# First layer's down projection of four quads as seven block products, x chunks in pairs, PSUM in two tiles of four banks

## Chip, core and metric

The kernel runs on one core of a Trainium2 chip. The metric is the device time of one execution in microseconds (us), as the median of three runs. The engines are named as in the profile: PE multiplies matrices and PEld loads its weights beside it, DVE and ACT work on vectors, POOL and SP are used here to issue transfers. PE's results land in PSUM, a memory of eight banks of 512 float32 words on each of 128 partitions; DVE or ACT read them from there (an "evacuation" below) into the on-chip buffer SBUF.

## What is computed

Two layers of a bidirectional encoder over 512 tokens of width 1024. Each layer has two attention branches fed by one input projection, and then a gated feed-forward part of hidden width 2816, which the change is about:

```python
for l in range(DEPTH):                       # DEPTH = 2
    h = rms_norm(x, attn_norm_g[l])
    z = jnp.einsum('bsd,dc->bsc', h, w_in[l])
    ...
    x = x + jnp.einsum('bsd,de->bse', mixed, w_out[l])
    h = rms_norm(x, ffn_norm_g[l])
    u = jax.nn.silu(jnp.einsum('bsd,df->bsf', h, w_gate[l])) * jnp.einsum('bsd,df->bsf', h, w_up[l])
    x = x + jnp.einsum('bsf,fd->bsd', u, w_down[l])
```

All is float32. Each product of matrices is made of three passes of the reduced type float32r: both operands are split in a high and a low part, and high x high, high x low and low x high are added up in PSUM.

## The kernel before

**How the work is tiled.** x lies with its features on partitions in eight chunks of 128 features x 512 tokens (`xT`), so a plain product has 128x128 weights and 512 tokens of moving data: three matmuls of 512 columns for each 128x128 weight block. In the feed-forward part the first 256 hidden features are done plainly (`pair_matmul`), and the other 2560 as five "quads" of 512. A quad's gate and up projections are made with seven block products instead of eight (2x2 blocks of 512 x 256 weights and 512 x 256 tokens, with sums of blocks ahead of the products and of results behind): `m_step` runs one product, 24 matmuls of 256 columns. The class `Quad` loads a quad's weights, makes the sums of weight blocks, and splits each in a high and a low part.

**The down projection.** In the first layer it is plain: `d_products` takes one chunk c of 128 output features and the four feature blocks of a quad, 12 matmuls of 512 columns with the tokens as moving data, and `add_x` adds the bank to `xT[c]`. Eight such steps make one quad. In the last layer it is made with seven block products too (`d_step`, letter "D"), with tokens on partitions: 12 matmuls of 512 columns for one product, evacuated by two additions. `chain_v` makes the sums and the split of the hidden blocks for it.

**What sets the order.** The whole program is unrolled by a planner: the kernel function runs `trunk` twice, once dry with a clock for each engine, to choose the places of the buffers and the order, and once to emit instructions. The main line (`layer`) emits PE's matmuls in order. Short chains (attention, splits) are emitted between them when their inputs are due (`Need`, `issue`). What follows a product, its evacuation among it, is put off with `soon` by 0.1 us of the planner's clock, and `tick` then emits it after the next three matmuls. `token_steps` and `ffn_steps` list the order of the steps in the last and in the first layer.

**PSUM.** `bank()` takes one bank's worth of words out of one tile of eight banks (`ARENAS`, kind `PS`); `Layout.pack` gives it a place after the dry run. The framework on which the kernel is built adds the waits between engines by itself, from what each instruction reads and writes in a tile. Attention holds at most four banks at once by a count of slots (`at_slots`); the other banks are used by the projections and by the feed-forward part. All calculating instructions are emitted through one helper, so the profile shows them with one line (L337), and buffers are named "arena".

Of the kernel before, what the change touches and what calls it, by code (L numbers as in the profile page):

```python
# [29 lines left out]
ARENAS = {F32: 21504, F32R: 31104, PS: 8 * 512}  # L30
# [197 lines left out]
def trunk(ctx: ExitStack, tc: tile.TileContext, a: dict, out: bass.AP, lay: Layout):  # L228
# [8 lines left out]
    def nm(s):  # L237
# [4 lines left out]
        k: (pb if k == PS else ar).tile([P, lay.WORDS if lay.dry else n], F32 if k == PS else k, tag=f"ar{i}", name=f"arena{i}")  # L242
# [21 lines left out]
    def bank():  # L264
        return buf([S], PS)
# [261 lines left out]
    def token_steps():  # L527

        steps = []
        for q in range(QUADS):  # L530
            ms = [("m", q, w, m) for w in ("w_gate", "w_up") for m in ORDER]
            ds = [("D", q - 1, m) for m in DORDER] if q else [("t", *x) for x in np.ndindex(2, NB)]
            for i, m in enumerate(ms):
                steps.append(m)
                for _ in range(i % 2 if q else 2 * (i >= 5)):
                    if ds:
                        steps.append(ds.pop(0))
        return steps + [("D", QUADS - 1, m) for m in DORDER]

    def ffn_steps():  # L540
        groups = [(0, 2)] + [(2 + 4 * i, 4) for i in range(QUADS)]
        steps = []
        for q in range(QUADS):
            ms = [("m", q, w, m) for w in ("w_gate", "w_up") for m in ORDER]
            ds = [("d", *groups[q], c) for c in range(KD)]
            for i, m in enumerate(ms):
                steps.append(m)
                if ds and i >= (1 if q else 5):
                    steps.append(ds.pop(0))
        return steps + [("d", *groups[-1], c) for c in range(KD)]  # L550
# [3 lines left out]
    def plan_ffn(l):  # L554
        plan_pair(a["w_gate"][l], 0, KD, on_engines=True)
        plan_pair(a["w_up"][l], 0, KD)
        down = a["w_down"][l]
        for step in ffn_steps() if l < DEPTH - 1 else token_steps():
            if step[0] == "m":
                _, q, w, m = step  # L560
                if m == ORDER[0]:
                    t = total[0]
                    early = 18.0 if q == 0 and w == "w_gate" else 0.0
                    col = 256 + 512 * q
                    srcs = [a[w][l][512 * h : 512 * h + 512, col : col + 512] for h in range(2)]
                    quads[l, q, w] = Quad(srcs, t - early, early > 0.0, l == DEPTH - 1)
# [3 lines left out]
            elif step[0] == "D":  # L570
                _, q, m = step
                if m == DORDER[0]:
                    f0 = 256 + 512 * q
                    srcs = [down[f0 + 256 * h : f0 + 256 * h + 256] for h in range(2)]
                    early = LEAD_LAST if q == QUADS - 1 else 0.0
                    quads[l, q, "w_down"] = Quad(srcs, total[0] - early, False, True)
                quads[l, q, "w_down"].due(m, total[0] - early)
                at_pos(total[0] - LEAD_V, lambda key=("go", q, m): done.add(key))
                total[0] += 4 * UNIT
# [78 lines left out]
    class Quad:  # L658
# [3 lines left out]
        def __init__(self, srcs, t, first, transfers):  # L662
# [5 lines left out]
            if not self.paced:  # L668
                at_pos(t - LEAD_PREP - LEAD_RAW, self.load)

        def load(self):
            k, n = self.shape
            wide = [buf([k, 2 * n]) for _ in range(2)]
            for t, src in zip(wide, self.srcs):
                Q.dma_start(t, src)
            (self.a11, self.a21), (self.a12, self.a22) = ((t[:, :, :n], t[:, :, n:]) for t in wide)
            self.s1 = buf(self.shape)
            if self.first:
                spawn(self.chain())
# [8 lines left out]
        def due(self, m, t):  # L688
            if self.first:
                at_pos(t - LEAD_PREP, lambda: done.add((self, m)))  # L690
            elif not self.paced:
                at_pos(t - LEAD_PREP, lambda: (self.sums(m), self.high(m)))
                at_pos(t - LEAD_PREP + 1.8, lambda: self.low(m))
# [24 lines left out]
        def source(self, m):  # L718
            if self.paced:
                at = {1: (1, 1), 2: (1, 2), 4: (2, 2), 7: (2, 1)}  # L720
                return self.blocks[at[m]] if m in at else self.s2 if m == 6 else self.s1
            return {1: self.a11, 2: self.a12, 3: self.a12, 4: self.a22, 5: self.s1, 6: self.a11, 7: self.a21}[m]

        def sums(self, m):
            add = lambda o, x, y: V.tensor_tensor(o, x, y, ALU.add)
            if self.paced:
# [24 lines left out]
        def low(self, m):  # L751
            src, h = self.parts[m]
            lo = buf(self.shape, F32R)
            if self.paced and m in MOVED or self.first and m not in (1, 2):
# [58 lines left out]
    def turn_over(n):  # L813

        ps = bank()
# [47 lines left out]
    ps = bank()  # L863
# [11 lines left out]
    def chain_tables():  # L875
# [4 lines left out]
        ps = bank()  # L880
# [66 lines left out]
    class Norm:  # L947
# [18 lines left out]
        def chain(self):  # L966
# [4 lines left out]
            ps = bank()  # L971
# [10 lines left out]
            ps = bank()  # L982
# [8 lines left out]
    def pair_matmul(parts, xh, xl, evac):  # L991

        ps = [bank(), bank()]
# [16 lines left out]
    def token_matmul(nrm, evac, begin=None):  # L1010

        ps = [bank() for _ in range(NB)]
# [87 lines left out]
    def turned(tiles, col, perm):  # L1100

        at_slots.take()
        ps = bank()
# [4 lines left out]
    def turned_back(tiles, col):  # L1108

        at_slots.take()  # L1110
        ps = bank()
# [98 lines left out]
    def head(g, q, k, v, bias, perm, init, sink, o_dst, in_a, key):  # L1210
# [6 lines left out]
        for j in range(NB):  # L1217
# [4 lines left out]
            ps = bank()  # L1222
# [25 lines left out]
        for i, (turns, n, products, ends) in enumerate(steps_):  # L1248
# [3 lines left out]
            pt = bank()  # L1252
# [12 lines left out]
            if po is None:  # L1265
                at_slots.take()
                po = bank()
# [47 lines left out]
    def start(nrm, k):  # L1315

        done.add(f"x{k}")
        ps = bank()
# [16 lines left out]
    def layer(l):  # L1335
# [26 lines left out]
        def chain_kv():  # L1362
# [4 lines left out]
            for t in (kt, vt):  # L1367
                yield Need("pe", [t], [at_slots])
                at_slots.take()
                ps = bank()  # L1370
# [219 lines left out]

        nrm = norms[2 * l + 1] = Norm(2 * l + 1)
# [24 lines left out]
        def chain_out():  # L1616

            yield Need(keys=["x_out", f"rows{nrm.i}"])
            for b in range(NB):
                xo.append(buf([D]))  # L1620
                for half in range(2):
# [3 lines left out]
                    ps = bank()  # L1625
# [92 lines left out]
        def quadrant(q, w, i, t, src, sign):  # L1718
# [10 lines left out]
            if last:  # L1729
                blocks[q, i, t] = g.rearrange("p (j n) -> p j n", j=2)  # L1730
                done.add(("u", q, i, t))
# [10 lines left out]
        def chain_v(q):  # L1742
# [7 lines left out]
            def low(m):  # L1750
# [5 lines left out]
                done.add(("v", q, m))  # L1756

            def go(m, i, t):
                yield Need(keys=[("u", q, i, t), ("go", q, m)])
# [41 lines left out]
        def m_step(q, w, m):  # L1801
            if m == 1:
                ps.clear()
                if w == "w_up" and last:
                    spawn(chain_v(q))
                elif w == "w_up":
                    us[q] = [(buf([2, S], F32R), buf([2, S], F32R)) for _ in range(2)]
                    u.extend((hs[:, j], ls[:, j]) for hs, ls in us[q] for j in range(2))
# [14 lines left out]
            def seed():  # L1823
                ps["b"] = bank()
# [10 lines left out]
            def seed_c():  # L1835
                ps["c"] = plus(bank())
# [33 lines left out]
        def t_step(half, b, wk):  # L1870
            o = bank()
# [13 lines left out]
        def d_step(q, m):  # L1885
            at = "D" if m in (1, 6, 7, 4) else "E"
            if m in (1, 5, 2):
                pd[at] = [bank() for t in range(2)]
# [4 lines left out]
            for t in range(2):  # L1893
                pieces = [(pd[at][t], slice(0, S))]
                if final and m == DORDER[-1] and t:
                    pieces = [(pd[at][t], slice(0, S // 2)), (bank(), slice(S // 2, S))]
# [21 lines left out]

        if last:
            fluid[0] = True  # L1920
            spawn(chain_out())
            for i, step in enumerate(token_steps()):
# [17 lines left out]
                else:  # L1940
                    _, q, m = step
                    yield ("v", q, m)
# [3 lines left out]
        steps_ = ffn_steps()  # L1946
        for i, step in enumerate(steps_[:-KD]):
            if step[0] == "m":
# [4 lines left out]
                yield from m_step(q, w, m)  # L1953
            else:
# [6 lines left out]
                o = bank()  # L1961
# [3 lines left out]
        norms[2 * l + 2] = Norm(2 * l + 2)  # L1965
        for c in range(0, KD, 2):
            wk = w_take()
            os_ = [bank(), bank()]
            for half in range(2):
                for j in range(2):  # L1970
                    fs = range(f0 + 2 * half, f0 + 2 * half + 2)
# [38 lines left out]
```

## Time and profile before

| | |
|---|---|
| median of three runs | 1364.15 us (1364.15 to 1364.66) |
| the profiled execution | 1363.46 us, span 1361.7 us |
| PE busy | 1355.1 us (100% of the span), 8008 matmul records |
| PEld | 1202.9 us (88%) |
| DVE | 961.3 us (71%) |
| ACT | 774.5 us (57%) |
| POOL | 310.3 us (23%) |
| DMA | 219.00 MB, mean 161 GB/s |
| clock granted to PE | full in all 40 slices of the span |

The span is the time from the first to the last instruction in the profile. "Busy" is the time in which the engine had at least one instruction under way; matmuls are pipelined, so a single one lasts longer than its distance to the next one. The profile names what ended an engine's idle time ("idle before <- releaser"). The stages of the span are, in us: attention and projections of the first layer 0 to 367, its feed-forward part 367 to 694, the same of the second layer 694 to 1045 and 1045 to 1362.

### The profile page before, as it was taken

The page shows a single profiled execution, that of the slowest core. Times are in us where ns is not written, and L with a number is a line of the kernel's source. Part 1 is how long each engine was busy: PE and PEld are TensorE (multiplying, and loading weights), DVE is VectorE, ACT ScalarE, POOL GpSimd, SP SyncE. Part 2 cuts the span into 40 slices and gives each one's busy share as a digit, 9 for nine tenths or more (in the row PEclk, how much of TensorE's full clock was granted, in tenths as well). Part 3 has the DMA queues.
Part 4 walks back from the last instruction along what each step waited for, and adds up shares of the span by engine and source line. Part 5 has one row for each costly group of instructions (what it writes and reads, how often), then busy time and mean ns, then how long its engine had stood idle before and what let it go on. Part 6 is the DMA issues. An engine that isn't in the chain of part 4 may idle for free.

```text
span 1361.7 us, 21050 instructions
## 1 busy us (share of the span) xinstructions
PE 1355.1 (100%) x8008; PEld 1202.9 (88%) x8008; DVE 961.3 (71%) x1778; ACT 774.5 (57%) x1244; POOL 310.3 (23%) x325
## 2 busy tenths in 40 slices
PE   9999999999999999999999999999999999999998
PEld 7888888888899999999988888888888999999997
DVE  6876878455976566575648758784559587878888
ACT  7477677534643443333544766775347556667572
POOL 5442222300211010102244422223002111011110
PEclk9999999999999999999999999999999999999999
DMA  9997888873866373736799879879647877595873
GB/s 235 197 169 133 149 163 161 170 201 99 152 155 150 101 189 96 193 69 140 138 204 193 157 134 169 160 141 188 171 120 147 201 179 180 161 247 132 219 171 99
DMA packets 193188, 219.00 MB, mean 161 GB/s; under 512 B 26160, under 2 KB 159712, under 8 KB 193088
## 3 DMA queue, kind: packets, MB, share of 16 engines
q0 software_dynamic: 118816, 142.59, 55.5%
q1 hardware_dynamic: 73776, 74.40, 18.4%
q8 instruction: 63, 1.03, 0.3%
q10 hardware_dynamic: 496, 0.67, 0.2%
q14 instruction: 37, 0.30, 0.1%
HBM read 183.02 MB, written 2.10 MB: 136 GB/s over the span
## 4 chain that ended last, share of the span: by engine, by line
PE 91%; DVE 3%; ACT 2%; DMA 1%; issue 1%; POOL 1%; SPq 0%; ACTq 0%; POOLq 0%
PE arena L337 91%; DVE arena L337 2%; ACT arena L337 2%; DMA arena<-in_w_in 1%; POOL arena L337 1%; DMA arena<-in_rel_bias_b 0%; DVE sm L337 0%; DMA arena<-in_x 0%; ACT L337 0%; SPq L337 0%; ACT sm L337 0%; DVE den L337 0%; ACT trig L337 0%; DVE rstd L337 0%; ACTq L337 0%
## 5 line engine op out<-in xcount | busy, mean ns | idle before, releaser
L337 PE MATMUL arena<-arena 128*128 128x256 f32 (+2 forms) x7466 | 1323.3, 338 | 0.6 <-DVE arena L337 0.4
L337 PEld LDWEIGHTS arena<-arena 128*128 128x128 f32 x7466 | 1142.7, 190 | 141.9 <-issue 0.7
L337 DVE TENSOR_TENSOR arena<-arena,arena 128x512 f32<-128x512 f32 (+6 forms) x701 | 537.9, 792 | 290.9 <-PE arena L337 222.6
L337 ACT CAST arena<-arena 128x1024 fp32r<-128x1024 f32 (+4 forms) x443 | 341.5, 792 | 270.3 <-DVE arena L337 204.5
L337 ACT ACTIVATE arena<-arena 128x1024 fp32r<-128x1024 f32 (+3 forms) x302 | 247.0, 838 | 131.3 <-PE arena L337 40.6
L337 POOL DMA_DIRECT2D arena<-in_w_in x163 | 162.9, 1399 | 298.4 <-ACT arena L337 286.3
L337 DVE TENSOR_TENSOR arena<-arena 128x1024 f32<-128x1024 f32 (+3 forms) x226 | 189.3, 853 | 2.3
L337 ACT COPY arena<-arena 128x512 f32<-128x512 f32 (+1 forms) x118 | 67.9, 583 | 81.0 <-PE arena L337 78.7
L337 POOL DMA_DIRECT2D arena<-in_w_down x52 | 54.6, 1239 | 256.1 <-ACT arena L337 169.7
L337 POOL DMA_DIRECT2D arena<-arena x52 | 48.2, 926 | 268.1 <-ACT arena L337 167.8
L337 ACT ACTIVATE arena<-arena,negm 128x256 f32<-128x256 f32 (+1 forms) x128 | 68.2, 533 | 18.2 <-DVE negm L337 16.3
L337 PE MATMUL arena<-cst,arena 128*128 128x128 f32 x472 | 72.0, 273 | 1.7 <-DMA arena<-in_x 1.1
L337 PEld LDWEIGHTS arena<-cst,arena 128*128 128x128 f32 x472 | 57.2, 140 | 11.3 <-DVE arena L337 1.9
L337 DVE CUSTOM_DVE_ANT_0 arena<-arena,cst,nsnk 128x256 f32<-128x256 f32 (+1 forms) x64 | 34.4, 548 | 33.0 <-PE arena L337 32.2
L337 DVE CUSTOM_DVE_ANT_0 arena<-arena,arena 128x256 f32<-128x256 f32 x64 | 26.3, 420 | 20.9 <-PE arena L337 20.5
L337 ACT ACTIVATE arena<-arena,vec2T 128x512 fp32r<-128x512 f32 x16 | 11.6, 726 | 47.5 <-DVE arena L337 47.5
L337 POOL DMA_DIRECT2D arena<-in_w_up x8 | 8.3, 1035 | 125.4 <-PE arena L337 92.7
L337 DVE TENSOR_SCALAR arena<-arena,sm 128x256 f32<-128x256 f32 (+1 forms) x88 | 29.6, 387 | 1.1
L337 POOL DMA_DIRECT2D arena<-in_w_proj_b x16 | 17.5, 1286 | 50.9 <-ACT arena L337 50.9
L337 DVE TENSOR_REDUCE sm<-arena 128x8 f32<-128x512 f32 (+1 forms) x32 | 17.4, 579 | 16.3 <-ACT arena L337 16.3
L337 ACT ACTIVATE arena<-arena,sm 128x256 f32<-128x256 f32 (+1 forms) x40 | 20.0, 521 | 7.8 <-DVE sm L337 7.7
L337 ACT ACTIVATION_READ_ACCUMULATOR arena<-arena,negm 128x1 f32 x128 | 24.1, 188 | 0.0
(62 smaller groups left out, 262.8 us busy)
## 6 DMA issues: line engine op xcount, KB each, us to landing
arena<-in_w_in POOLq DMA_DIRECT2D x99, 512.0 KB, 7.3
arena<-arena POOLq DMA_DIRECT2D x52, 512.0 KB, 6.9
arena<-in_w_down POOLq DMA_DIRECT2D x44, 512.0 KB, 6.7
arena<-in_w_in POOLq DMA_DIRECT2D x64, 256.0 KB, 6.8
arena<-in_w_gate SPq DMA_DIRECT2D x12, 1024.0 KB
arena<-in_w_gate SPq DMA_DIRECT2D x20, 512.0 KB
arena<-in_w_up SPq DMA_DIRECT2D x10, 1024.0 KB
arena<-in_w_up SPq DMA_DIRECT2D x20, 512.0 KB
```

Of the source, the lines that this page charges most:

```text
L337: f(*args, **kw)
```

## The change

Four things are changed together.

- The first layer's down projection of quads 0 to 3 is made of seven block products (letter "F", `f_step`). Features stay on partitions: one product is 24 matmuls of 256 columns with sums of hidden blocks as moving data, in two banks, each of which a subtraction or addition of 128 x 512 puts into a pair of x chunks. `chain_v` makes the hidden blocks and `Quad` the weight blocks, as the last layer has them. The first 256 features and the last quad of that layer stay plain.
- The quads' weights of the first layer, but for the first, are loaded block by block, and three of the seven low parts are made by transfers that add (`low_by_transfer`), as in the last layer.
- The chunks of the first layer's new x lie in pairs in one buffer (`xp`).
- PSUM is two tiles of four banks in place of one of eight: "mm" for the projections and part of the feed-forward part, "at" for attention and the rest of the feed-forward part.

The core of the diff (each other `bank()` becomes `at_bank()` in the chains of attention and in `Norm`, and `mm_bank()` in `pair_matmul`, `token_matmul`, `t_step` and `d_products`):

```diff
-ARENAS = {F32: 21504, F32R: 31104, PS: 8 * 512}
+ARENAS = {F32: 21504, F32R: 31104, "mm": 4 * 512, "at": 4 * 512}
...
-        k: (pb if k == PS else ar).tile([P, lay.WORDS if lay.dry else n], F32 if k == PS else k, tag=f"ar{i}", name=f"arena{i}")
+        k: (pb if isinstance(k, str) else ar).tile([P, lay.WORDS if lay.dry else n], F32 if isinstance(k, str) else k, tag=f"ar{i}", name=f"arena{i}")
...
-    def bank():
-        return buf([S], PS)
+    def mm_bank():
+        return buf([S], "mm")
+
+    def at_bank():
+        return buf([S], "at")
...
+            if q:
+                ds = [("D" if last else "F", q - 1, m) for m in DORDER]
+            else:
+                ds = [("t", *x) for x in np.ndindex(2, NB)] if last else [("d", 0, 2, c) for c in range(KD)]
...
-            self.paced = transfers and not first
...
                 if l < DEPTH - 1:
-                    V.tensor_tensor(xT[k], xT[k], ps, ALU.add)
+                    if j == 0:
+                        xp.append(buf([2, S]))
+                    V.tensor_tensor(xp[dp][:, j], xT[k], ps, ALU.add)
+                    xT[k] = xp[dp][:, j]
...
             if m in (1, 5):
-                ps[at] = bank()
+                ps[at] = at_bank()
...
             def seed():
-                ps["b"] = bank()
+                ps["b"] = mm_bank()
                 A.copy(ps["b"], o)
...
-                ps["c"] = plus(bank())
+                ps["c"] = plus(mm_bank())
...
+        def f_step(q, m):
+            at = "D" if m in (1, 6, 7, 4) else "E"
+            if m in (1, 5, 2):
+                pd[at] = [(mm_bank if at == "D" else at_bank)() for p in range(2)]
+            hi, lo = quads[l, q, "w_down"].parts[m]
+            h, lw = vs[q, m]
+            half, th = DBLOCK[m]
+            for p in range(2):
+                o = pd[at][p]
+                for j, k in np.ndindex(2, 2):
+                    oj, c = o[:, 256 * j : 256 * j + 256], slice(P * (2 * p + j), P * (2 * p + j) + P)
+                    mm(oj, hi[:, k, c], h[:, k], m in (1, 5, 2) and j == k == 0, False)
+                    mm(oj, hi[:, k, c], lw[:, k], False, False)
+                    mm(oj, lo[:, k, c], h[:, k], False, k == 1)
+                    tick(3 * 0.12)
+                    yield UNIT
+
+                def add(o=o, p=p):
+                    x = xp[2 * half + p][:, :, 256 * th : 256 * th + 256]
+                    ps = o.rearrange("p (j n) -> p j n", j=2)
+                    V.tensor_tensor(x, x, ps, ALU.add if half == 0 else ALU.subtract)
+
+                soon(add)
```

Outside the first layer's feed-forward part the order of the instructions on each engine is the same but for a handful that change places; what differs there is the banks and the waits. In the rows below, which are PE's order with the semaphores that an instruction waits for (`DVE_49`, `Activation_49`, and `DMA...` for transfers), arena0 and arena1 are SBUF (float32 and float32r). Before, `arena2_71` is PSUM; of the change, `arena2_71` is the tile "mm" and `arena3_72` the tile "at".

First place: PE in the middle of the output projection `w_out` of the first layer, where two banks take turns, 12 matmuls each. Before:

```order
L337 MATMUL arena2_71<-arena1_70 128x512 [waits Activation_49]
L337 MATMUL arena2_71<-arena1_70 128x512 [waits DVE_49]
L337 MATMUL arena2_71<-arena1_70 128x512 x13
L337 MATMUL arena2_71<-arena1_70 128x512 [waits Activation_49]
L337 MATMUL arena2_71<-arena1_70 128x512
```

The same place of the change:

```order
L340 MATMUL arena2_71<-arena1_70 128x512 [waits Activation_49]
L340 MATMUL arena2_71<-arena1_70 128x512 [waits DVE_49]
L340 MATMUL arena2_71<-arena1_70 128x512
L340 MATMUL arena2_71<-arena1_70 128x512 [waits DVE_49]
L340 MATMUL arena2_71<-arena1_70 128x512 x11
```

A wait for DVE now stands at the first matmul of the second bank's last 12: the operation it waits for reads the first bank.

Second place: PE in the first layer's feed-forward part, at quad 1's products with one step of the down projection between them. Before:

```order
L337 MATMUL arena2_71<-arena1_70 128x256 x21
L337 MATMUL arena2_71<-arena1_70 128x512 x12
L337 MATMUL arena2_71<-arena1_70 128x256 [waits Activation_49]
L337 MATMUL arena2_71<-arena1_70 128x256
L337 MATMUL arena2_71<-arena1_70 128x256 [waits DVE_49]
L337 MATMUL arena2_71<-arena1_70 128x256 x21
```

The first F step of the change (24 matmuls), and the product behind it:

```order
L340 MATMUL arena2_71<-arena1_70 128x256 [waits DVE_49]
L340 MATMUL arena2_71<-arena1_70 128x256
L340 MATMUL arena2_71<-arena1_70 128x256 [waits DMASW6_49]
L340 MATMUL arena2_71<-arena1_70 128x256 x12
L340 MATMUL arena2_71<-arena1_70 128x256 [waits DVE_49]
L340 MATMUL arena2_71<-arena1_70 128x256 x11
L340 MATMUL arena2_71<-arena1_70 128x256 [waits DVE_49]
L340 MATMUL arena2_71<-arena1_70 128x256 x20
```

12 matmuls of 512 columns became 24 of 256, and there are waits for DVE three matmuls into the second bank's half of the step and three matmuls into the next product: after each evacuation that `soon` puts there.

Third place: PE in the second layer's feed-forward part, one D step (12 matmuls of 512 columns) and the start of the product behind it, code that the diff leaves as it was but for the banks. Before:

```order
L337 MATMUL arena2_71<-arena1_70 128x512 [waits Activation_49]
L337 MATMUL arena2_71<-arena1_70 128x512 [waits DVE_49]
L337 MATMUL arena2_71<-arena1_70 128x512 x10
L337 MATMUL arena2_71<-arena1_70 128x256 [waits DVE_49]
L337 MATMUL arena2_71<-arena1_70 128x256
L337 MATMUL arena2_71<-arena1_70 128x256 [waits DMASW2_49]
L337 MATMUL arena2_71<-arena1_70 128x256 x21
```

The same step of the change:

```order
L340 MATMUL arena2_71<-arena1_70 128x512 [waits Activation_49]
L340 MATMUL arena2_71<-arena1_70 128x512 x2
L340 MATMUL arena2_71<-arena1_70 128x512 [waits Activation_49]
L340 MATMUL arena2_71<-arena1_70 128x512 x5
L340 MATMUL arena2_71<-arena1_70 128x512 [waits DVE_49]
L340 MATMUL arena2_71<-arena1_70 128x512 x2
L340 MATMUL arena2_71<-arena1_70 128x256 x2
L340 MATMUL arena2_71<-arena1_70 128x256 [waits DMASW1_49]
L340 MATMUL arena2_71<-arena1_70 128x256 [waits DVE_49]
L340 MATMUL arena2_71<-arena1_70 128x256 x20
```

The matmuls are the same; waits for ACT and DVE stand three matmuls into the step, three into its second bank and three into the next product.

More of the change, by code (lines that the diff above doesn't have):

```diff
@@ L525, in trunk, with ffn_steps @@
     DORDER = (1, 5, 6, 3, 7, 4, 2)
-    def token_steps():
+    def ffn_steps(l):
+        last = l == DEPTH - 1
         steps = []
@@ L531, in token_steps @@
             ms = [("m", q, w, m) for w in ("w_gate", "w_up") for m in ORDER]
-            ds = [("D", q - 1, m) for m in DORDER] if q else [("t", *x) for x in np.ndindex(2, NB)]
+            if q:
+                ds = [("D" if last else "F", q - 1, m) for m in DORDER]
+            else:
+                ds = [("t", *x) for x in np.ndindex(2, NB)] if last else [("d", 0, 2, c) for c in range(KD)]
             for i, m in enumerate(ms):
                 steps.append(m)
-                for _ in range(i % 2 if q else 2 * (i >= 5)):
+                for _ in range(i % 2 if q else (i >= 5) * (1 + last)):
                     if ds:
                         steps.append(ds.pop(0))
[L538 to L550, printed above, removed]
+        q = QUADS - 1
+        return steps + ([("D", q, m) for m in DORDER] if last else [("d", 2 + 4 * q, 4, c) for c in range(KD)])
     quads = {}
@@ L557, in plan_ffn @@
         down = a["w_down"][l]
-        for step in ffn_steps() if l < DEPTH - 1 else token_steps():
+        for step in ffn_steps(l):
             if step[0] == "m":
@@ L575, in plan_ffn @@
                     early = LEAD_LAST if q == QUADS - 1 else 0.0
-                    quads[l, q, "w_down"] = Quad(srcs, total[0] - early, False, True)
+                    quads[l, q, "w_down"] = Quad(srcs, total[0] - early, False)
                 quads[l, q, "w_down"].due(m, total[0] - early)
-                at_pos(total[0] - LEAD_V, lambda key=("go", q, m): done.add(key))
-                total[0] += 4 * UNIT
+                at_pos(total[0] - LEAD_V, lambda key=("go", l, q, m): done.add(key))
+                total[0] += 4 * UNIT if kind == "D" else 24 * 0.12
             elif step[0] == "t":
@@ L677, in load @@
             self.s1 = buf(self.shape)
-            if self.first:
-                spawn(self.chain())
+            spawn(self.chain())
         def fetch(self, *blocks):
@@ L718, in source @@
         def source(self, m):
-            if self.paced:
+            if not self.first:
                 at = {1: (1, 1), 2: (1, 2), 4: (2, 2), 7: (2, 1)}
@@ L725, in sums @@
             add = lambda o, x, y: V.tensor_tensor(o, x, y, ALU.add)
-            if self.paced:
+            if not self.first:
                 at = self.blocks
@@ L753, in low @@
             lo = buf(self.shape, F32R)
-            if self.paced and m in MOVED or self.first and m not in (1, 2):
+            if m not in (1, 2) if self.first else m in MOVED:
                 low_by_transfer(lo, src, h)
@@ L813, in turn_over @@
     def turn_over(n):
-        ps = bank()
+        ps = mm_bank()
         for _ in range(n):
@@ L862, in trunk @@
     turn_over(7)
-    ps = bank()
+    ps = at_bank()
     T.transpose(ps[:, :16], vec, ident[:16, :16])
@@ L879, in chain_tables @@
         at_slots.take()
-        ps = bank()
+        ps = at_bank()
         T.transpose(ps[:, :P], vec2, ident)
@@ L970, in chain @@
             at_slots.take()
-            ps = bank()
+            ps = at_bank()
             for b in range(NB):
@@ L981, in chain @@
             at_slots.take()
-            ps = bank()
+            ps = at_bank()
             for b in range(NB):
@@ L1010, in token_matmul @@
     def token_matmul(nrm, evac, begin=None):
-        ps = [bank() for _ in range(NB)]
+        ps = [mm_bank() for _ in range(NB)]
         if begin is not None:
@@ L1102, in turned @@
         at_slots.take()
-        ps = bank()
+        ps = at_bank()
         for b in range(NB):
@@ L1110, in turned_back @@
         at_slots.take()
-        ps = bank()
+        ps = at_bank()
         for b in range(NB):
@@ L1251, in head @@
             th_slots.take()
-            pt = bank()
+            pt = at_bank()
             for j, x, to in turns:
@@ L1317, in start @@
         done.add(f"x{k}")
-        ps = bank()
+        ps = at_bank()
         for b in range(NB):
@@ L1728, in quadrant @@
                 V.scalar_tensor_tensor(g, src, sign, g, ALU.mult, ALU.mult)
-            if last:
+            if last or q < QUADS - 1:
                 blocks[q, i, t] = g.rearrange("p (j n) -> p j n", j=2)
-                done.add(("u", q, i, t))
+                done.add(("u", l, q, i, t))
                 return
@@ L1755, in low @@
                 vs[q, m] = h, lo
-                done.add(("v", q, m))
+                done.add(("v", l, q, m))
             def go(m, i, t):
-                yield Need(keys=[("u", q, i, t), ("go", q, m)])
+                yield Need(keys=[("u", l, q, i, t), ("go", l, q, m)])
                 return blocks[q, i, t]
@@ L1803, in m_step @@
                 ps.clear()
-                if w == "w_up" and last:
+                if w == "w_up" and (last or q < QUADS - 1):
                     spawn(chain_v(q))
@@ L1870, in t_step @@
         def t_step(half, b, wk):
-            o = bank()
+            o = mm_bank()
             t = slice(P * b, P * b + P)
@@ L1887, in d_step @@
             if m in (1, 5, 2):
-                pd[at] = [bank() for t in range(2)]
+                pd[at] = [(mm_bank if at == "D" else at_bank)() for t in range(2)]
             hi, lo = quads[l, q, "w_down"].parts[m]
@@ L1953, in layer @@
                 yield from m_step(q, w, m)
+            elif step[0] == "F":
+                _, q, m = step
+                yield ("v", l, q, m)
+                yield from f_step(q, m)
             else:
@@ L1965, in layer @@
         norms[2 * l + 2] = Norm(2 * l + 2)
+        fluid[0] = False
         for c in range(0, KD, 2):
             wk = w_take()
-            os_ = [bank(), bank()]
+            os_ = [mm_bank(), mm_bank()]
             for half in range(2):
                 for j in range(2):
-                    fs = range(f0 + 2 * half, f0 + 2 * half + 2)
+                    fs = range(2 + 2 * half, 4 + 2 * half)
                     yield from d_products(os_[j], c + j, fs, wk[2 * half : 2 * half + 2], half == 0, half == 1)
```

38 lines of the change are left out of this document (18 added, 20 removed).

## Prediction

> **What bounds the kernel now.** I read the page first: busy shares, the chain that ended last, and the costliest groups.
>
> ```profile
> span 1361.7 us, 21050 instructions
> PE 1355.1 (100%) x8008; PEld 1202.9 (88%) x8008; DVE 961.3 (71%) x1778; ACT 774.5 (57%) x1244; POOL 310.3 (23%) x325
> ...
> PE 91%; DVE 3%; ACT 2%; DMA 1%; issue 1%; POOL 1%; SPq 0%; ACTq 0%; POOLq 0%
> ...
> L337 PE MATMUL arena<-arena 128*128 128x256 f32 (+2 forms) x7466 | 1323.3, 338 | 0.6 <-DVE arena L337 0.4
> ```
>
> PE is busy all the time, the chain runs through it for 91% of the span, and the 7466 main matmuls waited 0.6 us altogether before they could start. So nothing else bounds this kernel, no evacuation of PSUM holds PE up today, and two things alone can change the time: the work that PE is given, and waits that PE does not have now.
>
> Next I read the windows of the steady stages: one quad of the first layer's feed-forward part with its step of the down projection, a stretch of 168 matmuls of 256 columns without any of 512, one quad of the second layer, and the gate projections of the first layer.
>
> ```profile
> core 0: us, PE busy (x) PEld busy (x) DVE busy (x) ACT busy (x) POOL busy (x), PEclk, DMA share, GB/s
> 427.35:489.59 62.24, 62.24 (x434) 58.33 (x432) 38.79 (x42) 24.02 (x30) 8.12 (x8) 1.00 0.57 133
> 466.69:486.84 20.15, 20.15 (x169) 20.15 (x168) 17.22 (x20) 7.33 (x9) 2.05 (x2) 1.00 0.45 105
> 1109.20:1168.70 59.50, 59.50 (x421) 56.07 (x420) 48.51 (x58) 38.46 (x45) 7.71 (x9) 1.00 0.73 186
> 253.00:348.00 95.00, 95.00 (x422) 78.66 (x420) 52.40 (x71) 43.79 (x63) 12.91 (x13) 1.00 0.64 152
> ```
>
> The columns are the window, its length, then busy time and instructions of each engine, the granted clock, and the DMA. PE is gapless in all of them. 20.15 us / 168 = 0.120 us for a matmul of 256 columns; 95.00 / 420 = 0.226 us for one of 512.
>
> **Term A, PE's own work.** A quad of the first layer is 336 matmuls of 256 columns (14 products x 24) and 96 of 512 (8 chunks x 4 blocks x 3): the 432 weight loads of the first window, 62.24 us. With seven products of 24 in place of the 96 it is 504 matmuls of 256 columns, 504 x 0.1199 = 60.45 us. That saves 1.79 us a quad, 4 x 1.79 = 7.2 us for four. An eighth less of the 22 us of those 96 would be 2.7 us; the shorter matmuls, at more than half the distance of the long ones, take back the rest. It is the whole gain that the change can have.
>
> What comes with it on the other engines: for each of four quads seven splits of hidden blocks and their sums, four sums and seven splits of weight blocks, and 14 evacuations instead of 8. The second layer does all of this already, in the third window: DVE 48.51 us of 59.50, ACT 38.46, DMA share 0.73, and PE without a gap. The first layer has the same products in 60.45 us, so I cost these edits at nothing; they would cost only if DVE ran full, for which 11 us a quad are left. Pairs of x chunks in one buffer move no instruction. The three low parts that now come by adding transfers stand on the queues in the same third window, with PE fed.
>
> **Term B, the new waits.** The order shows something that the diff does not. With one PSUM tile of eight banks, each wait of PE for DVE or ACT that concerns PSUM was for an operation on the same bank. In the order of the change, with two tiles of four banks, I count 566 waits of PE for an evacuation, a seed or another operation of DVE or ACT that touches *another* bank of the same tile; before there are none. 376 are for DVE, 190 for ACT. By stage: first layer ahead of its feed-forward part 166, that part 119, second layer ahead of its feed-forward part 156, that part 125. In 387 of them (89, 102, 90, 106) the waiting matmul stands right behind the last matmul that the evacuation itself has to wait for, with nothing between; `soon` puts most evacuations three matmuls into the next step, and the fourth then waits. In the other 179 PE has work on the other tile in between.
>
> The price of one, from the groups by shape:
>
> ```profile
> L337 PE MATMUL arena<-arena 128*128 128x512 f32 x3582 | 866.8, 393 | 0.1
> L337 DVE TENSOR_TENSOR arena<-arena,arena 128x512 f32<-128x512 f32 x275 | 188.1, 687 | 228.8 <-PE arena L337 222.3 <-ACT arena L337 6.1
> L337 ACT COPY arena<-arena 128x512 f32<-128x512 f32 x86 | 49.2, 583 | 67.0 <-PE arena L337 66.5
> ```
>
> and from the timeline around two places where an engine did wait:
>
> ```profile
> 755.46 0.54 DVE L337 TENSOR_SCALAR arena<-arena,sm 128x256 f32<-128x256 f32 x1
> ...
> 756.04 0.14 PEld L337 LDWEIGHTS arena<-cst,arena 128*128 128x128 f32 x1 [0.32 <-DVE arena L337]
> 756.05 0.33 PE L337 MATMUL arena<-cst,arena 128*128 128x128 f32 x1
> ...
> 756.41 0.59 ACT L337 CAST arena<-arena 128x512 fp32r<-128x512 f32 x1
> ```
>
> ```profile
> 1057.36 0.53 PEld L337 LDWEIGHTS arena<-arena 128*128 128x128 f32 x4 [0.41 <-issue]
> 1057.39 0.59 PE L337 MATMUL arena<-arena 128*128 128x256 f32 x3 [0.24 <-DVE arena L337]
> ```
>
> A matmul of 512 columns ends 0.393 us after its start, 0.17 us after the next one could have started (0.226). The evacuation starts about 0.04 us after that end (756.38 to 756.41), takes 0.687 us on DVE or 0.583 on ACT, and PE's next weight load follows 0.05 us later (756.00 to 756.04). That is 0.17 + 0.04 + 0.69 + 0.05 = 0.95 us of idle PE for DVE, 0.84 for ACT; weighted 376 to 190, 0.91. After a stop the pipeline of weight loads is empty: the three matmuls of the last row take 0.59 us, where 0.12 + 0.12 + 0.28 = 0.52 would do without a stop. With these 0.07 us I take 1.0 us a wait (0.98).
>
> - 387 waits with nothing between: 387 x 1.0 = 387 us.
> - 179 with other work between: from 0 (evacuation done meanwhile) to 0.95 each. The 36 in the two feed-forward parts have a whole product of 24 matmuls (2.9 us) between, or nearly: nothing. The 143 in attention often wait for an operation that itself stands behind softmax work on DVE: 0.4 each, the middle, 57 us.
> - An evacuation can find its engine busy. The row above says that evacuations of this shape on DVE spent 222 of 229 idle us waiting for PE, so DVE mostly stands ready; but an operation of 128x1024 ahead of one lasts 1.22 us:
>
> ```profile
> L337 DVE TENSOR_TENSOR arena<-arena,arena 128x1024 fp32r<-128x1024 f32 x157 | 190.5, 1220 | 19.6 <-ACT arena L337 19.3
> ```
>
>  I add 0.1 us for each of the 387, 39 us; the ends are 0 and 0.35 (half such an operation, somewhat more often than every second time).
>
> **Sum.** 1361.7 - 7.2 + 387 + 57 + 39 = 1837.5 us of span. The median of the runs, 1364.15, stands 2.45 us above this profiled span, so 1840 us: slower by 35%. All stages share it: about 120 us in each layer ahead of its feed-forward part and 120 us in each feed-forward part, the one that the change leaves alone too. A quad of the second layer has some 20 such waits and goes from 59.5 to about 80 us.
>
> Bounds: the 387 alone at the bare 0.91 and 0 for all else give 1361.7 - 7.2 + 352 + 2.45 = 1709. All 566 at 1.0 with 0.35 of queue for the 387 give 1361.7 - 7.2 + 566 + 135 + 2.45 = 2058; that takes the worst of three things at once.
>
> **Rivals.**
>
> *The waits are met before PE gets there (faster).* A wait in the order costs nothing if the evacuation is over when the matmul is due, as with the true waits of today. The place is the fourth matmul of a step, the price then 0, and what is left is term A: 1364.15 - 7.2 = 1357 us. It decides at 0.95 us: between the last matmul that the evacuation needs and the one that waits for it there would have to be four matmuls of 512 columns or eight of 256 on the other tile. In 387 cases there are none, and the groups leave no way for an evacuation to take less than 0.58 us. It could hold only if the program on the chip did not have these waits. [...] But the order has them, and an engine does not pass a semaphore because the data would allow it. Chance 0.04.
>
> *The clock falls.* PE is granted the full clock in all 40 slices, with PE never idle for long:
>
> ```profile
> PEclk9999999999999999999999999999999999999999
> ...
> 0.00:5.00 5.00, 3.57 (x15) 3.24 (x15) 0.18 (x1) 1.48 (x2) 4.13 (x14) 1.00 0.56 147
> ```
>
> In the first 5 us PE was busy for 3.57 only, 71%, and the clock was 1.00; the change leaves PE about 74% busy (1355 of 1840), in gaps of 1 us. If the clock nevertheless fell to half for a quarter of PE's work, that would add a quarter of the 1355 us of PE's busy time, 339, and give about 2180. [...] Chance 0.05.
>
> *Evacuations queue.* If the chains of DVE and ACT hold each other up through the same false order (a DVE read of one bank behind an ACT read of another), a wait costs 1.5 us and more: 566 x 1.5 = 849 us, 2206 in all. Against it: PE stands still meanwhile, so DVE falls from 71% to about 53% busy and its queue empties. Chance 0.06 above 2000.
>
> *The price is too high.* In attention several waits follow each other within 1.5 us; where PE has just waited for one evacuation, the next is over sooner. If half of attention's 89 + 90 waits with nothing between cost nothing, and the other terms are at their low end, it is 1709 - 90 x 0.91 = 1627. Chance 0.06 below 1700.
>
> **How the numbers follow.** The forecast, 1700 to 2000 us, has 0.79; the rivals have 0.04, 0.05, 0.06 and 0.06. The range of 1700 to 2000 holds the low bound and most of the way to the high one, which needs three worst cases together. A measurement here can tell about 0.2% from no change. Faster by more than that is the first rival alone, 0.04; within 0.2% would need a few of the waits to cost just 7 us together, 0.01; slower 0.95.
>
> **What would show it.** PE's idle time before its matmuls, 0.6 us now, should be several hundred us, released by DVE and by ACT about two to one, with about 1 us each. The gate projections (253 to 348) should take some 25 us longer though their matmuls are the same; a quad of the second layer should show 420 matmuls in about 80 us. The first layer's quad should have 504 weight loads, and PE's sum of distances without the waits should be 7 us lower. The granted clock should stay at 1.00. I am wrong if PE is still gapless (then the waits are met, or not there), or if its gaps are led by DMA or by the missing parts of a quad's hidden blocks.

## Result and profile after

The changed kernel takes 1903.4 us (median of 4 runs, 1892.95 to 1907.61) against 1364.41 us before: a ratio of 1.394, interval 1.388 to 1.400. That is slower by 539 us and inside the predicted range, 63 us above the predicted 1840.

The page of the change, with the lines that answer to those of before (busy times, granted clock in 40 slices, chain, and the costliest group of PE):

```profile
span 1891.2 us, 22076 instructions
...
PE 1514.4 (80%) x8296; PEld 1230.4 (65%) x8296; DVE 1007.1 (53%) x1835; ACT 839.5 (44%) x1307; POOL 308.8 (16%) x332
...
PEclk9998799999999999999999989989999999999999
...
PE 12%; DVE 3%; ACT 1%; issue 1%; DVEq 0%
...
L340 PE MATMUL arena<-arena 128*128 128x256 f32 (+1 forms) x7754 | 1454.5, 341 | 341.5 <-DVE arena L340 235.6
```

The chain could be followed back for only the last 17% of this span. PE was busy for all of the span and is now busy for 80% of it. Its main matmuls waited 0.6 us in all before, and wait 341.5 now. DVE and ACT work as long as the edits make them (1007 and 840 us) and have become idler: nothing has taken PE's place as the bound. PE and the evacuations wait for each other in turn. The clock, shown as full in every slice before, is lower in four of the 40 slices here (7 or 8 tenths), and 0.975 in the mean.

The waits of PE in the change (what waited for what: us in total, times, longest):

```profile
PE arena L340 <- DVE arena L340: 251.7, 287, 3.9
PE arena L340 <- ACT arena L340: 107.3, 151, 1.5
PE arena L340 <- DVE negm L340: 8.8, 13, 1.2
```

DVE and ACT release PE about two to one, in 451 waits that show as idle time. One of them, in the timeline of the second layer's feed-forward part (start, length, engine, operation, in brackets the idle time ahead and its releaser):

```profile
1548.79 1.34 PE L340 MATMUL arena<-arena 128*128 128x256 f32 x7
...
1550.16 0.60 ACT L340 ACTIVATE arena<-arena 128x512 f32<-128x512 f32 x1 [2.81 <-PE arena L340]
...
1550.81 0.76 PEld L340 LDWEIGHTS arena<-arena 128*128 128x128 f32 x4 [1.12 <-ACT arena L340]
1550.81 0.97 PE L340 MATMUL arena<-arena 128*128 128x512 f32 x3 [0.69 <-ACT arena L340]
```

The first piece ends with three matmuls of 512 columns of the next step, the last of which starts at 1549.74 and ends at 1550.13. ACT begins its evacuation 0.03 us later, needs 0.60 us, and PE's weight load follows 0.05 us behind it. From 1549.74 to 1550.81 it is 1.07 us where matmuls of 512 columns stand 0.2265 apart: 0.84 us lost, the price that the prediction took for ACT. DVE has work of its own here until 1550.68.

The windows that the prediction named, the first layer's gate projections and a quad of the second layer (length; busy time and instructions of PE, PEld, DVE, ACT, POOL; granted clock; DMA):

```profile
373.84:497.98 124.14, 102.99 (x421) 76.87 (x420) 53.10 (x71) 45.31 (x65) 13.39 (x14) 1.00 0.51 121
1542.49:1623.38 80.89, 64.92 (x421) 55.54 (x420) 49.39 (x58) 38.36 (x45) 7.61 (x9) 1.00 0.57 137
```

The same 420 matmuls took 95.00 and 59.50 us before. In both windows the clock is full, so these 29 and 21 us are waits alone. By the starts of the same matmuls in both traces, the four stages (first layer ahead of its feed-forward part, that part, and the same of the second layer, parted at 345, 695 and 1039 us of before) went from 343.8, 350.5, 344.2 and 318.6 us to 493.3, 461.0, 491.4 and 440.5.

### The profile page after: what moved, and what is told of

Read it like the earlier page. It is cut to its first block, busy times and chain, and to the rows that moved or that the text cites. A ratio compares the mean times of both kernels' runs of the same rounds, so it can differ in the third digit from the quotient of the medians.

```text
span 1891.2 us, 22076 instructions
## 1 busy us (share of the span) xinstructions
PE 1514.4 (80%) x8296; PEld 1230.4 (65%) x8296; DVE 1007.1 (53%) x1835; ACT 839.5 (44%) x1307; POOL 308.8 (16%) x332
## 5 line engine op out<-in xcount | busy, mean ns | idle before, releaser
L340 PE MATMUL arena<-arena 128*128 128x256 f32 (+1 forms) x7754 | 1454.5, 341 | 341.5 <-DVE arena L340 235.6
L340 PEld LDWEIGHTS arena<-arena 128*128 128x128 f32 x7754 | 1165.3, 193 | 602.1 <-DVE arena L340 316.2
L340 DVE TENSOR_TENSOR arena<-arena,arena 128x512 f32<-128x512 f32 (+6 forms) x726 | 553.6, 780 | 591.4 <-PE arena L340 444.9
L340 ACT CAST arena<-arena 128x512 fp32r<-128x512 f32 (+3 forms) x483 | 375.9, 802 | 515.1 <-DVE arena L340 348.8
L340 ACT ACTIVATE arena<-arena 128x1024 fp32r<-128x1024 f32 (+2 forms) x325 | 271.0, 853 | 133.6 <-PE arena L340 60.4
L340 DVE TENSOR_TENSOR arena<-arena 128x1024 f32<-128x1024 f32 (+3 forms) x250 | 213.9, 870 | 2.0
L340 POOL DMA_DIRECT2D arena<-arena x91 | 80.6, 886 | 696.7 <-ACT arena L340 597.3
L340 PE MATMUL arena<-cst,arena 128*128 128x128 f32 x472 | 81.0, 295 | 30.3 <-DVE arena L340 16.1
L340 POOL DMA_DIRECT2D arena<-in_w_down x20 | 23.2, 1210 | 40.6 <-ACT arena L340 40.4
L340 DVE SCALAR_TENSOR_TENSOR arena<-arena 128x512 f32<-128x512 f32 (+2 forms) x38 | 25.9, 681 | 0.6
```

Of the source, the lines that this page charges most:

```text
L340: f(*args, **kw)
```

## Experiments

The **waits theory** is that of the prediction: PE stops for operations that touch another bank of the same PSUM tile. Its rivals are that the loss comes from the new down projection, from having only four banks in a group, or from the clock. All experiments but the fifth start from the changed kernel.

### 1. The new down projection alone

One tile of eight banks again, and each bank taken from all eight; the rest of the change stays. No wait for another bank is left in the order.

```diff
-ARENAS = {F32: 21504, F32R: 31104, "mm": 4 * 512, "at": 4 * 512}
+ARENAS = {F32: 21504, F32R: 31104, "mm": 8 * 512}
...
     def at_bank():
-        return buf([S], "at")
+        return buf([S], "mm")
```

This kernel leaves a part of the result out: by its order, two matmuls of the first layer's quad 0 overwrite a partial sum which ACT had copied into their bank, where they should add to it (no trace shows this). The matmuls are as many as in the change.

> The change with PSUM left as one tile of eight banks, any bank for any use. In its order no wait of PE is for another bank (566 in the change). If the new waits are the whole loss (theory W), only term A is left: 1364.4 - 7.2 = 1357 us, ratio 0.995, PE gapless, clock 1.00. If the block products, the pairs of chunks or the block loads cost by themselves (rival F), part of the 539 us stays: well above 1364.

Measured: 1358.4 us, ratio 0.996 (0.995 to 0.997), clock 1.000. Without the two tiles the loss is gone, and a small gain is left.

### 2. The two groups as halves of one tile

Banks and groups as in the change, but both groups are cut from one tile of eight banks. Again no wait for another bank.

```diff
+    whole = pb.tile([P, lay.WORDS if lay.dry else 8 * 512], F32, tag="ar2", name="arena2")
+    arenas["mm"] = whole if lay.dry else whole[:, : 4 * 512]
+    arenas["at"] = whole if lay.dry else whole[:, 4 * 512 :]
```

> The change with its two groups of four banks kept as halves of one tile of eight banks. Same groups, same steps, no wait for another bank. W: within 3 us of e1_f_only, about 1358 us (a few evacuations in attention now stand 0.7 us ahead of a true reuse of their bank, where 0.95 is needed: some 10 x 0.2 us). Rival G (four banks a group are too few): 20 us or more above e1_f_only.

Measured: 1360.6 us, ratio 0.9973 (0.9962 to 0.9984), clock 1.000. It computes what the change computes, on the same banks, with the same matmuls in PE. Its busy times, and PE's waits:

```profile
PE 1350.2 (99%) x8296; PEld 1212.7 (89%) x8296; DVE 998.0 (73%) x1835; ACT 833.7 (61%) x1307; POOL 308.6 (23%) x332
```

```profile
PE arena L344 <- DVE arena L344: 1.8, 3, 1.4
...
PE arena L344 <- DVE negm L344: 0.7, 2, 0.5
```

368 us of PE's waits have become 2.5. The whole loss, 1903.4 - 1360.6 = 543 us, thus hangs on PSUM being two tiles of the framework, and neither on the banks nor on the groups. This version does without all of these waits: DVE and ACT evacuate banks here while PE goes on writing others, and PE is 99% busy.

This version also shows term A by itself. First the stretch of before from quad 1's first step to the last plain steps of the first layer, then the same stretch of this version, which is 2040 matmuls of 256 columns:

```profile
415.97:667.80 251.83, 251.83 (x1753) 236.18 (x1752) 155.99 (x170) 99.73 (x122) 35.61 (x35) 1.00 0.58 135
```

```profile
419.17:663.96 244.79, 244.79 (x2042) 244.79 (x2040) 196.32 (x231) 153.62 (x181) 34.42 (x40) 1.00 0.72 170
```

PE stands in neither, and the difference is 7.04 us. DVE is at 80% and ACT at 63% of the stretch and hold nothing up.

### 3 and 4. One group coarse, the other bank by bank

Experiment 3 keeps "mm" as one tile of four banks and makes each bank of "at" a tile of its own (278 waits for another bank, 222 for DVE and 56 for ACT). Experiment 4 does it the other way round, with `SINGLE = ('mm',)` (323 waits, 175 and 148).

```diff
+    SINGLE = ('at',)
...
+    banks_of = {
+        k: [pb.tile([P, S], F32, tag=f"b{k}{i}", name=f"bank_{k}{i}") for i in range(ARENAS[k] // S)]
+        for k in SINGLE
+        if not lay.dry
+    }
...
+        if dtype in banks_of:
+            return banks_of[dtype][x // S][:, x % S : x % S + n]
```

> The change with each bank of the group at as a tile of its own; the group mm stays one tile of four. 278 waits for another bank are left in the order (222 for DVE, 56 for ACT). W at the 0.96 us a wait of the change ((1903 - 1357) / 566): 1357 + 267 = 1624 us, between 1570 and 1670. If the granted clock falls because stops are frequent, it should be nearer 1.00 than the change's 0.97; if some other thing lowers it, it stays at 0.97.

> The change with each bank of the group mm as a tile of its own; the group at stays one tile of four. 323 waits for another bank are left (175 for DVE, 148 for ACT). W: 1357 + 323 x 0.96 = 1667 us, between 1610 and 1720, mostly in attention. Granted clock as for e3_mm_coarse: nearer 1.00 if the density of stops sets it.

Measured: 1650.7 us (clock 0.993) and 1636.6 us (clock 0.969), 290 and 276 us above experiment 2: 1.04 and 0.85 us for each wait. The groups by shape of the third (the "mm" tile is "arena", the single banks are "bank_at"), then of the fourth:

```profile
L349 PE MATMUL arena<-arena 128*128 128x512 f32 x3024 | 787.7, 403 | 152.1 <-DVE arena L349 118.8 <-ACT arena L349 31.5 <-DMA arena<-in_w_in 0.9
L349 PE MATMUL arena<-arena 128*128 128x256 f32 x2304 | 305.6, 286 | 62.2 <-DVE arena L349 59.2 <-ACT arena L349 2.7
L349 PE MATMUL bank_at<-arena 128*128 128x256 f32 x2124 | 287.5, 285 | 0.2 <-DVE negm L349 0.2
```

```profile
L349 PE MATMUL bank_mm<-arena 128*128 128x512 f32 x3024 | 759.0, 403 | 0.1
L349 PE MATMUL arena<-arena 128*128 128x256 f32 x2124 | 313.9, 294 | 105.6 <-DVE arena L349 50.4 <-ACT arena L349 35.2 <-ACT bank_mm L349 13.7
L349 PE MATMUL bank_mm<-arena 128*128 128x256 f32 x2304 | 286.5, 284 | 0.2
```

The idle time sits in each case at the matmuls into the coarse tile, and the others wait 0.2 us, as before the change. Both groups carry about half. The clock is another matter: it falls hardly at all with the "mm" tile (0.993) and clearly with the "at" tile (0.969), though 278 and 323 waits are not far apart. So the count of the stops alone does not explain these two; experiment 8 follows that.

### 5. The kernel before with the two tiles alone

```diff
-ARENAS = {F32: 21504, F32R: 31104, PS: 8 * 512}
+ARENAS = {F32: 21504, F32R: 31104, "mm": 4 * 512, "at": 4 * 512}
...
-        ps = [bank(), bank()]
+        ps = [mm_bank(), mm_bank()]
```

> The kernel before with one edit: PSUM in two tiles of four banks, each bank asked from the group that the change gives it. The first layer's down projection stays plain. By the order this has 545 waits of PE for DVE or ACT on another bank (the change has 566). Waits theory: the loss does not need the new down projection; 1364 + 545 x 0.96 = about 1887 us (1850 to 1920), the stages as long as in the change but for some us in the first layer's feed-forward part. Rival, that the new down projection brings a good part of the loss in its own stage: under 1800 us.

Measured: 1890.6 us (1888.25 to 1894.49), ratio 1.386 (1.383 to 1.389), clock 0.966. The same two windows as above:

```profile
371.67:495.55 123.88, 102.70 (x422) 76.59 (x420) 53.11 (x71) 45.03 (x64) 13.16 (x14) 1.00 0.51 119
1530.37:1611.27 80.90, 64.93 (x421) 55.51 (x420) 49.39 (x58) 38.47 (x45) 7.71 (x9) 1.00 0.56 137
```

124 and 81 us, as in the change. The two tiles cost the kernel before 526 us with no new matmul in it, so the new down projection isn't needed for the loss.

### 6. Four tiles of two banks

The diff is that of experiment 3 with tiles of two banks, for both groups. 330 waits for another bank are left.

```diff
+        k: [pb.tile([P, 2 * S], F32, tag=f"b{k}{i}", name=f"bank_{k}{i}") for i in range(ARENAS[k] // S // 2)]
...
+            return banks_of[dtype][x // (2 * S)][:, x % (2 * S) : x % (2 * S) + n]
```

> The change with its two groups as two tiles of two banks each (four tiles). By the order 330 waits for another bank are left, 219 for DVE and 111 for ACT. Waits theory: 1360.6 + 330 x 0.95 = about 1675 us (1630 to 1710), so the loss goes with the number of such waits. Rival, that what costs is the division of PSUM into two halves as such (a bank that comes free too late in its group): the groups are the same as in the change, so near 1900 us.

Measured: 1614.6 us (1612.90 to 1615.23), 254 us above experiment 2, or 0.77 us a wait: below the expected 1630. The waits of PE:

```profile
PE bank_mm L349 <- DVE arena L349: 94.2, 100, 4.3
PE bank_at L349 <- DVE arena L349: 35.2, 43, 2.2
PE bank_at L349 <- ACT arena L349: 29.7, 45, 1.7
```

The loss goes with the waits and not with the groups, which are the same as in the change. Where the expectation was off is their mix. Of these 330 waits 164 have no other matmul between what the evacuation needs and the matmul that waits, and they cost 1.05 us each; the other 166 cost 0.22 (worked out as for the change, below). With fewer banks in a tile there is more often other work in between.

### 7. Each bank a tile of its own

As experiment 3, for both groups. No wait for another bank.

> The change with each of the eight banks a tile of its own, the two groups kept. By the order no wait for another bank. Waits theory: as with one tile of eight banks, 1358 to 1363 us, clock 1.00. Rival (groups of four banks are themselves too few): 1400 us or more.

Measured: 1360.3 us (1358.94 to 1360.52), ratio 0.9969 (0.9957 to 0.9980), clock 1.000; PE 99% busy. So tiles of one bank and a tile of all eight cost nothing, tiles of four banks 543 us, tiles of two 254. Groups of four banks are enough. Experiments 2 and 7 are the versions that beat both kernels, by about 4 us against before.

### 8. What lowers the clock

Behind the last step of experiment 2 stands a probe that is no part of the computation:

```diff
...
+    def burst(n):
+        for _ in range(n):
+            T.matmul(ps, w[:, :P], w, start=True, stop=True)
+
+    for n, rounds in ((1, 32), (2, 28), (3, 24), (4, 20)):
+        burst(72)
+        for _ in range(rounds):
+            burst(n)
+            A.copy(out_, ps)
+    burst(72)
```

> The version with one tile of eight banks, and behind its last step a probe that is no part of the computation: 72 matmuls of 512 columns in a row; 32 rounds of one such matmul, each held up until ACT has copied the bank; 72 in a row; 28 rounds of two; 72; 24 rounds of three; 72; 20 rounds of four; 72. A round should take 0.84 + 0.2265 n us: 1.07, 1.30, 1.52 and 1.75 us, with PE streaming 21, 35, 45 and 52% of it; the probe adds some 230 us. [...]

The windows of the probe: the rounds of one matmul ahead of and behind the clock's fall, those of two likewise, those of three and those of four (the column ahead of the last two is the granted clock):

```profile
1378.30:1381.20 2.90, 1.37 (x4) 0.37 (x2) 0.00 (x0) 1.27 (x3) 0.00 (x0) 1.00 0.00 0
1382.00:1424.00 42.00, 22.76 (x29) 8.07 (x29) 0.00 (x0) 16.68 (x29) 0.00 (x0) 0.50 0.00 0
...
1443.00:1449.50 6.50, 3.51 (x11) 1.35 (x9) 0.00 (x0) 2.34 (x4) 0.00 (x0) 1.00 0.00 0
1450.00:1495.00 45.00, 28.13 (x46) 11.57 (x46) 0.00 (x0) 13.53 (x24) 0.00 (x0) 0.50 0.00 0
1514.20:1554.70 40.50, 22.97 (x74) 11.52 (x72) 0.00 (x0) 14.06 (x24) 0.00 (x0) 1.00 0.00 0
1571.20:1609.60 38.40, 23.81 (x82) 13.33 (x80) 0.00 (x0) 11.70 (x20) 0.00 (x0) 1.00 0.00 0
```

This version ran once, in 1628.95 us: the probe added 268 us where some 230 were expected, as its rounds are longer and two series ran at half clock. At full clock the rounds took 1.17, 1.46, 1.69 and 1.93 us. With 0.2265 us for a matmul, PE streamed 19, 31, 40 and 47% of the time. At 19 and 31% the clock fell to half, 3 and 6.5 us after the series began, and stayed there until the next row of matmuls; at 40 and 47% it stayed full. Between two rounds PE is idle for 0.73 us at most, in all four series. So the falls in the first two series came with no idle stretch of PE longer than that.

## Why the prediction was right, and where it was off

The sum was 1837.5 us of span; the profiled run has 1891.2, 54 us more. To size the terms, each matmul of the trace was set beside its place in PE's order, and what its distance from the one before it exceeds the steady one (0.2265 us for 512 columns, 0.12 for 256, 0.172 for 384, 0.109 for the rest) was added up by the kind of wait.

**What bounds the kernel, and that the two tiles bring waits.** Right, and shown by experiments 2 and 5: the waits come and go with the tiles.

**Term A.** 7.2 us forecast, 7.04 found in its stretch (experiment 2). "I cost these edits at nothing" was not quite right: experiment 2's span is 1358.8 where 1361.7 - 7.2 = 1354.5 was due. A single stop in quad 0 is part of these 4 us, where before there was none of this size:

```profile
373.25 0.54 PEld L344 LDWEIGHTS arena<-arena 128*128 128x128 f32 x4 [1.60 <-DVE arena L344]
373.25 0.62 PE L344 MATMUL arena<-arena 128*128 128x256 f32 x3 [1.40 <-DVE arena L344]
```

What brings this stop was not followed. The first layer's stage ahead of it is also 1.6 us longer (345.4 against 343.8), and that comes from the first 10 us and not from the change. Matmuls of the same forms there, three rows of before and then three of experiment 2:

```profile
0.99 3.35 PE L337 MATMUL arena<-trig 128*128 128x128 f32 x14 [0.99 <-POOL trig L337]
...
6.16 0.83 PE L337 MATMUL arena<-trig 128*128 128x128 f32 x6
7.10 1.22 PE L337 MATMUL arena<-arena 128*128 128x512 f32 x4
```

```profile
6.67 1.49 PE L344 MATMUL arena<-trig 128*128 128x128 f32 x6
7.81 2.05 PE L344 MATMUL arena<-arena 128*128 128x512 f32 x4
...
10.23 1.18 PE L344 MATMUL arena<-arena 128*128 128x512 f32 x4
```

Matmuls of 512 columns stand 0.427 us apart in the second of these rows of experiment 2, and about 0.23 apart in the third: PE ran at about half clock until 10 us. In before only the first row is slow: its matmuls stand 0.213 apart, and those of the second row 0.112. The trace's record of the clock begins at 4.9 us in before and at 10.1 in experiment 2, and the views count the time ahead of it as full clock. By 20 us experiment 2 is 1.7 us behind before. The record begins at 4.5 to 5.0 us in four of the ten traces and at 9.1 to 10.3 in the other six, and kernels with the change are in both groups.

**Term B, its three parts.** The 566 waits stand at 561 matmuls. At 387 of them there is no matmul between, and they lost 388 us, 1.00 each: 0.97 at the 368 where the operation itself waited for PE, and 1.71 at the 19 where it stood behind another operation of its engine. The matmuls right behind the waiting ones lost 51 us more over all 561, 0.09 each, where the prediction had 0.07 for the refill of the weight loads. Together 1.09 a wait, where the prediction had 1.0 and 0.1 for a busy engine. The 174 with work between lost 53 us, 0.30 each, against 57 us forecast; nearly all of it in attention, as forecast. The sum is 388 + 51 + 53 = 492 us against 387 + 57 + 39 = 483. The two feed-forward stages grew by 110.5 + 5.6 (what term A took there, 350.5 to 344.9 in experiment 2) = 116 and by 121.9, where "120 us in each" was forecast; a quad of the second layer takes 80.9, "about 80" forecast; the gate projections gained 29 instead of 25.

**The step that failed** is the one to "The granted clock should stay at 1.00." The trace was called to witness for it by a misread window: the first 5 us of before, shown with a clock of 1.00, are the ones whose matmuls stand 0.213 us apart (under term A), so PE ran at about half clock in them and the record of the clock had not begun. Nor were all of PE's gaps such "of 1 us": two stops of the change last 3.9 and 3.7 us. The stages ahead of the feed-forward parts grew by 149.5 and 147.2 us instead of 120, of which the waits are 134 and 126, and the clock fell there: 0.96 in the mean from 0 to 497 and from 960 to 1457 us of the change, where the two feed-forward parts show 0.99. One place in the second layer's attention:

```profile
1157.20:1160.60 3.40, 1.76 (x10) 1.05 (x9) 1.76 (x6) 1.27 (x4) 0.00 (x0) 1.00 0.03 8
1160.60:1164.00 3.40, 3.40 (x9) 2.81 (x10) 1.80 (x7) 1.55 (x3) 1.36 (x2) 0.50 0.00 0
```

In the first of these stretches PE started matmuls worth about 1.4 of 3.4 us, and it was never idle for more than 1.1 us; in the second it runs without a gap, and matmuls of 512 columns stand 0.43 apart. The profiled run has 95.6 us at half clock. The matmuls that started in them would have taken 42 us at the steady distances, so at most 42 us were lost by it: 15, 5, 16 and 6 in the four stages. The four runs agree on the size: 1892.95 us at a mean clock of 0.975 and 1907.61 at 0.964 are 14.7 us for 0.011, which for the 0.025 that the profiled run lacks would be 33 us. With 9 us from the waits, 4 by which experiment 2 misses its sum, and some 33 to 42 from the clock, that is 46 to 55 of the 54 us. The rival itself ("half for a quarter of PE's work", 2180 us) was not what happened: no run shows a quarter of PE's work at half clock. The profiled run shows half clock for matmuls worth 42 us, where PE is busy for 1350 in experiment 2, and the price was a tenth of the rival's 339 us.

**The other rivals.** The waits are not met in time: the faster case would have needed the program to be without them, and that is experiments 2 and 7. The evacuations hardly queue: 1.00 us was lost where the bare price is 0.91. The price was not too high: in attention, too, waits with nothing between cost 1.02 us in the first layer and 0.99 in the second.

What stays open is why the framework keeps the banks of an eight-bank tile apart and those of a four-bank or two-bank tile not; the runs show only that it does.

## What to carry to other kernels

A PSUM tile is also the unit by which waits may be set: after any change to how banks are grouped, compare the waits in PE's order, not only the matmuls, and look for a wait on an operation that touches another bank. The gapless PE of this kernel paid the whole round trip for each of them, the tail of the last matmul and the evacuation, 1.00 us at the 387 places where no other matmul stands between and 0.09 more right behind, and it added up across stages that the change was not about. Where groups of banks are wanted, cut them from one tile or make each bank its own, as fits the framework (1360.6 and 1360.3 us here, against 1903.4), and look at the order again.

## What the hardware showed that was not expected

The granted clock fell to 0.50 though no stop within PE's work was longer than 3.9 us. The clock's record in the trace of the change has 18 falls within PE's work; the stretches at half clock last from 3.4 to 17.1 us, 95.6 us in all. Two of the falls follow the stops of 3.9 and 3.7 us; in the 3.4 us ahead of the other 16 PE is never idle for more than 2.2 us at a time. Experiment 4 has no stop of PE above 2.1 us and still 102 us at half clock. In experiment 8 the series of two matmuls fell with PE streaming 31% of the time and idle for 0.73 us at most, and the series of three and four, at 40 and 47% with stops no longer, stayed at 1.00. What sets the fall is not shown.

The trace of the change also tells where it happens: some 31 of the 42 us were lost in attention, which has 322 of the 566 waits, and the feed-forward parts, with the other 244, lost the rest. Why attention loses more to the clock for each wait is not shown.
